# Attention block 0: two halves of one score tile and one transpose tile, side-by-side transposed blocks, and a bias table built head by head

## The chip, the cores and the metric

The kernel runs on one core of a Trainium2 chip, in one launch. Its engines work from separate instruction streams: PE (matmul and transpose), PEld (the weight loads that go with it), DVE and ACT (elementwise work and the only readers of PE's output), POOL, and SP, which in this kernel issues most DMAs. The metric is the device time of one execution in microseconds (us); lower is better.

## The reference

One layer of a hybrid block, 2048 tokens of width 1024, all in float32. One normalised input is projected once; a quarter of the columns goes to a state-space mixer, the rest are q, k and v of 8 heads of 64. The attention sees the token's own chunk of 64 and the 8 chunks before it, with a bias by clipped distance.

```python
h = rmsnorm(x, norm_mix_g[l])
proj = h @ w_in[l]                         # u_ssm (512) | q (512) | k (512) | v (512)
y_ssm = s5_mixer(u_ssm, ...)               # scan over 2048 tokens, 32 groups, 64 complex states
...
rel = jnp.arange(BAND)[None, :] - LEFT_CHUNKS * CHUNK - jnp.arange(CHUNK)[:, None]
idx = jnp.clip(rel, -MAX_REL, MAX_REL) + MAX_REL
bias = rel_bias.astype(jnp.float32)[:, idx]
scores = jnp.einsum('bnqhd,bnkhd->bhnqk', qc, kb).astype(jnp.float32) / math.sqrt(HEAD_DIM)
scores = scores + bias[None, :, None, :, :]
scores = jnp.where(valid[None, None, :, None, :], scores, -1e30)
probs = jax.nn.softmax(scores, axis=-1)
out = jnp.einsum('bhnqk,bnkhd->bnqhd', probs.astype(v.dtype), vb)
```

Both outputs are normalised, joined, projected by `w_out` and added to `x`; a SwiGLU feed-forward layer and a last normalisation follow.

## The kernel before

Float32 accuracy is had from pairs: each operand is split into a high part and a low rest, and a product takes three matmuls (`mm3`, L79). Splitting a weight block is one ACT cast and one DVE or POOL subtraction (L155).

**The first phase** (`u_phase`) projects `u_ssm` for the four token blocks of 512 in the order 1, 2, 3, 0. Its loop variable `n` counts them; step `n` first issues the loads for a block (`prep`: eight `xt` tiles of the transposed input, L441, each split by ACT at L443 and DVE at L444; four rows of `x` for the norm, L450), then runs groups of 24 matmuls, eight tiles by three, on it. `prep` at `n = 2` is the block whose operand tiles are called `raw`, `w`, `xt`, `hi0x` to `hi2x`. The prologue of the state-space part is interleaved.

**The bias table.** `S["nbm"]` lies in DRAM, for each of the 8 heads 128 rows of 640 floats. One DMA from DRAM to DRAM builds it (L522, tile name `nbms<-nbs`), row by row from a one-dimensional list of each head, each row shifted by one float; two more DMAs (L525) overwrite the two masked corners of 64x64 of every head with 1e30. The table is issued at `n = 1`, the corners at `n = 3`. Later each head's 128x640 piece is loaded as the tile `nb` (L801, two buffers), the next head's at the third of a head's four steps.

**The attention phase** (`att_phase`) runs 128 steps: 4 token blocks `sb` x 4 head pairs x 2 heads x 4 query parts `qp` of 128. In each step stand, in this order, the scores of the step (`sc`, L79), the transposes of the step before (`pt`, L82), the value product of a finished head (`pj`), and filling work: generators called units that a table paces over the steps. Units are the projections of q and k (`qk_unit`), of v (`v_unit`), the operands of the next block (`hT_unit`, loads `xt` at L696 with `XB` buffers, product at L706, split at L707 and L708), and 8 `ssm_unit`s in a row, each of them: loads of `U`, `Bst`, `Tm`, `Vm`; matmuls `pj<-U,Bst`; ACT copies into `X` (L574); a scan on POOL (L588 to L600); the copy `XG<-X` issued by POOL (L622); matmuls `pj<-U,Tm` and `pj<-XG,Vm`; ACT copies (L632); eight stores `y<-X` (L635).

A score step is: PE writes `sc`, DVE adds the bias and takes the running minimum (`s<-sc,nb`, then `mn`, both L830), ACT takes the exponential (L833). PE then transposes `s` into `pt`; ACT copies it to `pth` (L848), and DVE makes the rest `ptl` (L849), which the value product reads. In token block 0 step `qp` has only `qp + 1` key blocks, numbered 4 to `qp + 4`; each is put at place `kb % 5` of `pt` and `pth`, so key block 4 is at place 4 and the others at 0 and up, and the copy takes two instructions each on ACT and DVE when `qp > 0`.

In token block 0 the projection weights are loaded in 512 KB pieces (`raw<-in_w_qk`, `raw<-in_w_v`, L675), split, and written back split as 1 MB pieces (`wss<-w`, L686) for the later blocks. `q2h`, `q2l`, `ks` are partition moves and stores of q and k (L750, L751, L756); `v` leaves its PSUM tile at L785 (ACT) and L786 (DVE).

**What sets the order.** Matmuls and transposes stand in the order of the program, pinned by `keep_in_program_order`. ACT, DVE, POOL and SP are ordered by a scheduler with its own estimate; an instruction that is pinned keeps its place among the pinned ones of its engine. SP takes its stream strictly in turn: a DMA whose wait is not over holds all DMAs behind it. Every SP DMA also uses one of eight completion semaphores in rotation and waits until the DMA eight places ahead has landed.

## Time and profile before

| what | value |
|---|---|
| time, median of 3 runs | 2354.85 us (2350.14 to 2355.02) |
| the profiled execution: its own time / its span | 2354.0 us / 2352.2 us |
| mean granted PE clock | 0.970 |
| PE busy, share of the span | 2204.0 us, 94% |
| PEld, DVE, ACT, POOL busy | 1853.1, 1468.7, 1001.3, 1136.5 us |
| DMA, all queues | 434.92 MB, mean 185 GB/s |

The first phase takes the first 140 us or so of the span, the attention phase goes to about 815 us, and the rest is the feed-forward part, which the change does not touch. All times quoted below are in us from the start of the span. In rows of a timeline the first number is the start and the second the duration; in square brackets stands how long the engine sat idle before it and what ended that. In rows of waits: total us, times, longest. A window's row gives its length and, engine by engine, the busy time in it and the number of instructions, then the granted PE clock, the busy share of the DMA engines and GB/s.

### The profile page before, as it was taken

The page shows a single profiled execution, that of the slowest core. Times are in us where ns is not written, and L with a number is a line of the kernel's source. Part 1 is how long each engine was busy: PE and PEld are TensorE (multiplying, and loading weights), DVE is VectorE, ACT ScalarE, POOL GpSimd, SP SyncE. Part 2 cuts the span into 40 slices and gives each one's busy share as a digit, 9 for nine tenths or more (in the row PEclk, how much of TensorE's full clock was granted, in tenths as well). Part 3 has the DMA queues.
Part 4 walks back from the last instruction along what each step waited for, and adds up shares of the span by engine and source line. Part 5 has one row for each costly group of instructions (what it writes and reads, how often), then busy time and mean ns, then how long its engine had stood idle before and what let it go on. Part 6 is the DMA issues. An engine that isn't in the chain of part 4 may idle for free.

```text
span 2352.2 us, 30719 instructions
## 1 busy us (share of the span) xinstructions
PE 2204.0 (94%) x10712; PEld 1853.1 (79%) x10712; DVE 1468.7 (62%) x2229; ACT 1001.3 (43%) x1666; POOL 1136.5 (48%) x1280
## 2 busy tenths in 40 slices
PE   8977799999997899989999998999999989999996
PEld 6766688898986788768888887788888868888886
DVE  6745645656555855746775668766645365579676
ACT  4435545555546642333333334433333343345332
POOL 3237644356551432465555557655555364345442
PEclk9989999999998999989999999999999989999998
DMA  8967776776644434743554646554423287465551
GB/s 275 299 203 251 213 205 178 206 213 189 187 139 135 157 117 148 264 143 117 188 171 157 231 169 243 191 199 165 170 89 119 75 310 261 169 211 184 204 179 72
DMA packets 225331, 434.92 MB, mean 185 GB/s; under 512 B 43480, under 2 KB 70152, under 8 KB 218072
## 3 DMA queue, kind: packets, MB, share of 16 engines
q1 hardware_dynamic: 220312, 418.79, 54.1%
q0 software_dynamic: 4864, 14.17, 2.0%
q8 instruction: 84, 1.38, 0.2%
q14 instruction: 71, 0.58, 0.1%
HBM read 292.88 MB, written 132.15 MB: 181 GB/s over the span
## 4 chain that ended last, share of the span: by engine, by line
PE 57%; DVE 4%; issue 1%; DMA 1%; POOL 1%; ACT 1%; SPq 0%; DVEq 0%; ACTq 0%; POOLq 0%
PE X L79 19%; PE ps L79 17%; PE Y L79 9%; PE big L79 7%; PE W L79 5%; DVE sa L1527 1%; DVE lo L155 1%; DMA lo<-hc 0%; POOL c L155 0%; POOL lo L155 0%; POOL sa L1098 0%; DVE hd L155 0%; DMA hd<-wc 0%; DVE S L1346 0%; ACT hi L155 0%
## 5 line engine op out<-in xcount | busy, mean ns | idle before, releaser
L79 PE MATMUL X<-hi,c 128*128 128x512 f32 x1408 | 450.4, 390 | 8.0 <-POOL c L155 4.0
L79 PE MATMUL ps<-hd,hd 128*128 128x512 f32 (+1 forms) x1968 | 435.1, 384 | 8.0 <-DVE hd L155 4.5
L79 PEld LDWEIGHTS ps<-hd,hd 128*128 128x128 f32 x1968 | 361.4, 191 | 80.4 <-DVE hd L155 4.9
L155 POOL TENSOR_TENSOR c<-S,c 128x512 fp32r<-128x512 f32 x176 | 252.8, 1438 | 245.2 <-ACT c L155 242.9
L79 PEld LDWEIGHTS X<-hi,c 128*128 128x128 f32 x1408 | 264.9, 188 | 65.5 <-POOL c L155 4.4
L155 POOL TENSOR_TENSOR hd<-hd 128x1536 fp32r<-128x1536 f32 (+1 forms) x53 | 188.2, 3556 | 211.2 <-ACT hd L155 196.0
L79 PE MATMUL X<-lo,c 128*128 128x512 f32 x704 | 274.4, 390 | 0.0
L155 POOL TENSOR_TENSOR c<-raw,c 128x512 fp32r<-128x512 f32 x132 | 188.1, 1425 | 130.6 <-ACT c L155 100.1
L155 ACT CAST hd<-hd 128x1536 fp32r<-128x1536 f32 (+1 forms) x106 | 147.3, 1392 | 227.6 <-DMA hd<-hq 162.8
L79 PE MATMUL Y<-hi,c 128*128 128x512 f32 x704 | 228.1, 395 | 14.1 <-DVE u L1368 14.1
L1492 DVE TENSOR_TENSOR acc<-acc,ps 128x512 f32<-128x512 f32 x196 | 129.2, 682 | 89.9 <-PE ps L79 89.8
L79 PEld LDWEIGHTS Y<-hi,c 128*128 128x128 f32 x704 | 134.1, 190 | 44.0 <-DVE u L1368 15.8
L830 DVE CUSTOM_DVE_ANT_0 s<-sc,nb 128x640 f32<-128x640 f32 (+4 forms) x128 | 94.5, 738 | 115.7 <-PE sc L79 104.5
L588 POOL TENSOR_TENSOR st<-X,a 128x128 f32<-128x128 f32 (+2 forms) x136 | 46.7, 343 | 247.2 <-ACT X L574 237.1
L79 PE MATMUL big<-m,woh 128*128 128x512 f32 x512 | 163.5, 401 | 0.2 <-DVE yr L1034 0.2
L79 PE MATMUL pf<-hi,w 128*128 128x512 f32 x416 | 151.8, 416 | 9.0 <-ACT w L155 4.6
L155 ACT CAST c<-S 128x512 fp32r<-128x512 f32 x176 | 109.3, 621 | 114.0 <-PE Y L79 59.5
L79 PEld LDWEIGHTS X<-lo,c 128*128 128x128 f32 x704 | 132.4, 188 | 27.3
L1364 ACT COPY u<-X 128x512 f32<-128x512 f32 x132 | 77.0, 584 | 180.2 <-PE X L79 180.2
L155 ACT CAST c<-raw 128x512 fp32r<-128x512 f32 x132 | 82.1, 622 | 152.6 <-PE Y L79 83.0
L79 PE MATMUL Y<-lo,c 128*128 128x512 f32 x352 | 138.4, 393 | 0.0
L155 DVE TENSOR_TENSOR hd<-hd 128x1536 fp32r<-128x1536 f32 (+1 forms) x53 | 111.6, 2107 | 34.3 <-ACT hd L155 33.9
(450 smaller groups left out, 4701.4 us busy)
## 6 DMA issues: line engine op xcount, KB each, us to landing
w<-wss SPq DMA_DIRECT2D x36, 1024.0 KB, 5.6
hq<-g SPq DMA_DIRECT2D x140, 256.0 KB, 2.1
hd<-hq SPq DMA_DIRECT2D x42, 768.0 KB, 4.5
hd<-wc SPq DMA_DIRECT2D x42, 768.0 KB, 6.1
raw<-in_w_gate SPq DMA_DIRECT2D x44, 512.0 KB, 3.7
raw<-in_w_up SPq DMA_DIRECT2D x44, 512.0 KB, 4.1
wc<-px SPq DMA_DIRECT2D x66, 256.0 KB, 3.1
wss<-w SPq DMA_DIRECT2D x12, 1024.0 KB, 5.9
```

The costliest lines, as they stand in the source:

```text
L79: return self.tc.keep_in_program_order(self.tc.nc.tensor.matmul(*a, **b))
L155: return nc.scalar.copy(hi, raw), (lo_eng or nc.gpsimd).tensor_tensor(lo, raw, f32(hi), op=ALU.subtract)
L588: eng.tensor_tensor(t[:, :, :, :n], src, ar, op=ALU.mult)
L830: nc.vector.tensor_tensor_reduce(s[:, :nk].rearrange("p (a b) -> p a b", a=nch), ps[:, :nch, :half], hd.nb[:, nk - 1 :: -1].rearrange("p ( ...
L1364: nc.scalar.copy(u[:], ps[:])
L1492: V.tensor_tensor(a, a, ps[:], op=ALU.add)
L1527: (nc.gpsimd if m else nc.vector).tensor_tensor(self.sa[m][:, :n], self.sa[m][:, :n], t[:, :n], op=ALU.add)
```

## The change

1. In token block 0 all score steps use one two-bank tile `sc` and take its halves by turns (`qp % 2`); likewise one tile `pt` of eight 128x128 places, of which a step uses one half. Before, each step took a new `sc` and a new `pt` from pools with one buffer.
2. In token block 0 the transposed blocks lie side by side (`place`: key block 4 at place 0), so one ACT and one DVE instruction empty a step's `pt`: 24 instructions fewer on each of ACT and DVE. PE and POOL have as many instructions as before.
3. The bias table is built by heads: heads 0 to 2 in one DMA at `n = 2` of the first phase with their corners at `n = 3`; each of heads 3 to 7 by one DMA at step 0, 4, 8, 12, 16 of the attention phase, and its two corner DMAs two steps later. All are pinned in program order on SP. There are 15 more SP DMAs.
4. The attention's pool `aa` lays out `pth`, `ptl` and six `q2h`, `q2l` buffers first, so `nb` and other tiles lie at other addresses. `corner` moves to a pool that lives longer.
5. The product of `hT_unit` (L706 before) is pinned on DVE.

```diff
+def pinned(k, out, in_):
+    k.tc.keep_in_program_order(k.nc.sync.dma_start(out, in_))
+
+def table(k, S, h0, h1):
+
+    if h0 < H:
+        pinned(k, S["nbm"][h0:h1], bass.AP(S["nb"].tensor, S["nb"].offset + 768 * h0 + 1, [[768, h1 - h0], [1, P], [1, 640]]))
+
+def corners(k, S, h0, h1):
+
+    if h0 < H:
+        for m in range(2):
+            pinned(k, S["nbm"][h0:h1, m * 64 : m * 64 + 64, m * 576 : m * 576 + 64].rearrange("h p c -> p h c"), S["corner"][:].unsqueeze(1).to_broadcast([64, h1 - h0, 64]))
...
             prep(b)
-            if n == 1:
-                corner = k.t(p1, "corner", [64, 64])
-                nc.gpsimd.memset(corner[:], 1e30)
-                nc.sync.dma_start(S["nbm"][:], bass.AP(S["nb"].tensor, S["nb"].offset + 1, [[768, H], [1, P], [1, 640]]))
-            if n == 3:
...
+            if n > 1:
+                (table, corners)[n - 2](k, S, 0, 3)
...
-                nc.vector.scalar_tensor_tensor(xt[:], xt[:], k.gm[:, q : q + 1], S["rsn"][:, ts], op0=ALU.mult, op1=ALU.mult)
+                k.tc.keep_in_program_order(
+                    nc.vector.scalar_tensor_tensor(xt[:], xt[:], k.gm[:, q : q + 1], S["rsn"][:, ts], op0=ALU.mult, op1=ALU.mult))
...
+        two = {}
+
+        def place(sb, kb):
+            return kb % 5 if sb else kb - 4
...
-            ps = k.t(psum2, "sc", [P, 2, 512])
+            if sb:
+                ps = k.t(psum2, "sc", [P, 2, 512])[:]
+            else:
+                if h == qp == 0:
+                    two["sc"], two["pt"] = k.t(psum2, "sc", [P, 2, 512]), k.t(psum, "pt", [P, 8, P], bufs=1)
+                ps = two["sc"][:, qp % 2 : qp % 2 + 1]
...
-            pt = k.t(psum, "pt", [P, 5, P], bufs=1)
+            pt = k.t(psum, "pt", [P, 8, P], bufs=1)[:] if sb else two["pt"][:, qp % 2 * 4 : qp % 2 * 4 + 4]
...
-            runs = [(0, 5)] if sb else ([(4, 5)] if qp == 0 else [(4, 5), (0, qp)])
-            for a, b in runs:
-                nc.scalar.copy(pth[:, a:b, qp, :], pt[:, a:b, :])
-                nc.vector.tensor_tensor(ptl[:, a:b, qp, :], pt[:, a:b, :], f32(pth[:, a:b, qp, :]), op=ALU.subtract)
+            n = 5 if sb else qp + 1
+            nc.scalar.copy(pth[:, :n, qp, :], pt[:, :n, :])
+            nc.vector.tensor_tensor(ptl[:, :n, qp, :], pt[:, :n, :], f32(pth[:, :n, qp, :]), op=ALU.subtract)
...
+        for n in "hl":
+            k.t(aa, f"pt{n}", [P, 5, 4, P], F32R)
+        for n in "hl":
+            for _ in range(3):
+                k.t(aa, f"q2{n}", [P, SB], F32R, bufs=3)
...
+            if s % 4 == 0:
+                table(k, S, s // 4 + 3, s // 4 + 4)
+            if s % 4 == 2:
+                corners(k, S, s // 4 + 3, s // 4 + 4)
```

PE's order is the same row for row. In the rows that follow, numbers behind a tile's name count its uses and differ between the two kernels; a lane `DMAHW..` in a wait is one of SP's eight completion semaphores, `DVE_49` and the like are the engines' own. `x2` stands for two such instructions in a row.

SP in the first phase, where the loads of `n = 2` begin; before:

```order
L450 DMA w_151<-in_x 128x1024
L450 DMA w_152<-in_x 128x1024 x2
L522 DMA nbms_69<-nbs_70 1024x1x640
L441 DMA xt_715<-in_xp 128x512
L441 DMA xt_719<-in_xp 128x512
L441 DMA xt_723<-in_xp 128x512
L441 DMA xt_727<-in_xp 128x512
L450 DMA w_151<-in_x 128x1024
```

and after:

```order
L458 DMA xt_714<-in_xp 128x512
L458 DMA xt_718<-in_xp 128x512
L458 DMA xt_722<-in_xp 128x512
L458 DMA xt_726<-in_xp 128x512
L467 DMA w_153<-in_x 128x1024 x2
L467 DMA w_154<-in_x 128x1024
L458 DMA xt_730<-in_xp 128x512
L467 DMA w_154<-in_x 128x1024
L458 DMA xt_734<-in_xp 128x512
L399 DMA nbms_69<-nbs_70 384x1x640
L458 DMA xt_738<-in_xp 128x512
L458 DMA xt_742<-in_xp 128x512
```

The loads of `n = 2` stood behind the whole table; now six of the eight stand ahead of a table of three heads, and two behind it.

SP at the start of the attention phase, where the first `nb` is loaded; before:

```order
L756 DMA ks_68<-lo2x_1313 128x512
L675 DMA raw_1591<-in_w_qk 128x1024
L686 DMA wss_75<-w_1585 128x2048
L801 DMA nb_1542<-nbms_69 128x640
L801 DMA nb_1629<-nbms_69 128x640
L550 DMA U_1688<-u_64 16x16x64 x8
```

and after:

```order
L768 DMA ks_68<-lo2x_1313 128x512
L399 DMA nbms_69<-nbs_70 128x640
L813 DMA nb_1551<-nbms_69 128x640
L686 DMA raw_1601<-in_w_qk 128x1024
L399 DMA nbms_69<-corner_108 64x64 x2
L813 DMA nb_1640<-nbms_69 128x640
L697 DMA wss_75<-w_1595 128x2048
L561 DMA U_1697<-u_64 16x16x64 x8
```

The first `nb` stood behind a 512 KB load and a 1 MB store; now it stands behind the table piece of head 3, and the load and the store come after it.

SP at the end of the first `ssm_unit`, where the weights of the last `qk_unit` of block 0 are loaded (`raw`, its q and its k piece); before:

```order
L756 DMA ks_68<-k_415_1940 128x512
L756 DMA ks_68<-k_418_1943 128x512
L675 DMA raw_2437<-in_w_qk 128x1024
L675 DMA raw_2442<-in_w_qk 128x1024
L801 DMA nb_2468<-nbms_69 128x640
L696 DMA xt_2513<-in_xt 128x512
L696 DMA xt_2515<-in_xt 128x512
L686 DMA wss_75<-w_2436 128x2048
L696 DMA xt_2597<-in_xt 128x512
L550 DMA U_2446<-u_64 16x16x64
L635 DMA y_65<-X_2378 16x4x256 x8
L550 DMA U_2446<-u_64 16x16x64 x7
```

and after:

```order
L399 DMA nbms_69<-nbs_70 128x640
L646 DMA y_65<-X_2347 16x4x256 x8
L686 DMA raw_2402<-in_w_qk 128x1024
L686 DMA raw_2407<-in_w_qk 128x1024
L561 DMA U_2411<-u_64 16x16x64 x8
L561 DMA Bst_2420<-bsts_71 128x512
L561 DMA Tm_2422<-kts_80 16x4x128 x8
L561 DMA Vm_2431<-vs_72 128x4x128
L399 DMA nbms_69<-corner_108 64x64 x2
L813 DMA nb_2435<-nbms_69 128x640
L707 DMA xt_2478<-in_xt 128x512
L707 DMA xt_2480<-in_xt 128x512
```

The two weight loads, the bias piece of head 5 and the first `xt` loads of the next block stood ahead of the eight stores `y`; now the weights stand behind the stores, and the bias piece and the `xt` loads also behind all loads of the second `ssm_unit`. In the same way the two weight loads of the second `v_unit` (`raw<-in_w_v`) stood ahead of the store `ya_s<-ya` of the first head pair, and now stand behind it.

On PE the second score step of block 0 waits for DVE in both kernels (before `[waits DVE_49,PE_49]`, after `[waits DVE_49]`), and the count it waits for belongs to the same DVE instruction, the running minimum `mn` of the step before, although the second step now writes the other half of the tile. The same holds for the steps and transposes that follow in block 0.

More of the change, by code (lines that the diff above doesn't have):

```diff
@@ L868, in pv_head @@
                 for m, px in ((0, pth), (1, ptl)):
-                    k.ta.matmul(yp[:, a * P : b * P], vt, px[:, kb % 5, a:b, :].rearrange("p a b -> p (a b)"),
+                    k.ta.matmul(yp[:, a * P : b * P], vt, px[:, place(sb, kb), a:b, :].rearrange("p a b -> p (a b)"),
                                      start=n == 0 and m == 0, stop=n == len(kbs) - 1 and m == 1)
@@ L1618, in block_kernel @@
             S["sw"] = k.t(p, "sw", [P, 3, 2, NPR])
+            S["corner"] = k.t(p, "corner", [64, 64])
+            nc.gpsimd.memset(S["corner"][:], 1e30)
             with tc.tile_pool(name="apf", bufs=2, space=bass.MemoryType.PSUM, reuse_waits="tile") as k.pfs:
```

5 lines of the change are left out of this document (1 added, 4 removed).

## The prediction

> **What bounds the kernel now.** The chain that ended last comes first, since it says which engine sets the end:
>
> ```profile
> PE 57%; DVE 4%; issue 1%; DMA 1%; POOL 1%; ACT 1%; SPq 0%; DVEq 0%; ACTq 0%; POOLq 0%
> ```
>
> PE carries it, so the change counts by what it does to PE's waits. PE's order is unchanged, and the change lies in the first 350 us. I therefore read PE's waits there, the first phase (0 to 130, first row) and then the attention's start (130 to 340):
>
> ```profile
> PE ps L79 <- ACT raw L443: 10.4, 2, 7.4
> ...
> PE sc L79 <- DVE mn L830: 13.3, 1, 13.3
> PE pj L79 <- DMA XG<-X: 6.2, 3, 4.7
> PE pt L82 <- DVE ptl L849: 5.3, 5, 1.9
> ```
>
> One wait of 13.3 us for a score step stands out; the rest are small, and the row of `XG` is a scan on POOL, which the change leaves alone. Behind this stretch PE is nearly full (window; busy time of PE second), so time that is won or lost in it is not taken up later:
>
> ```profile
> 340.00:500.00 160.00, 152.88 (x944) 138.25 (x943) 94.12 (x165) 87.59 (x172) 89.00 (x234) 0.98 0.66 198
> ```
>
> **Part 1: the first phase, about -6 us.** The whole table is issued at 36.37 and the loads of the next block behind it; SP's timeline, then ACT's and PE's:
>
> ```profile
> 36.37 0.79 SPq L522 DMA_DIRECT2D nbms<-nbs  x1
> 37.50 16.53 SPq L441 DMA_DIRECT2D xt<-in_xp  x4
> ...
> 63.95 1.38 ACT L443 ACTIVATE raw<-xt,g_mix 128x512 fp32r<-128x512 f32 x2 [14.58 <-DMA xt<-in_xp]
> ...
> 53.79 0.39 PE L79 MATMUL ps<-hi,wul 128*128 128x512 f32 x1
> ...
> 61.27 0.39 PE L79 MATMUL ps<-hi,wul 128*128 128x512 f32 x1
> 64.73 0.50 PE L79 MATMUL ps<-raw,wuh 128*128 128x512 f32 x1 [3.08 <-ACT raw L443]
> ...
> 74.80 1.05 PE L79 MATMUL pp<-ident,no 128*128 128x128 f32 x8
> ```
>
> The first load issued behind the table at 37.50 is used at 63.95, 26.5 us later; ACT was idle 14.6 us for it. From 53.79 to 61.27 PE makes 33 steps, 0.227 us each. The group of 24 on the new block takes from 61.5 to 74.8, 13.3 us, against 24 x 0.227 = 5.4: it loses 7.9. Without a table ahead the loads land long before 61. But two of the eight stand behind a table of three heads. The nearest row for a load with no table ahead is this one of the loads issued from 64 to 90:
>
> ```profile
> DMA to landing us min/median/max: 3.2/5.3/8.0
> ```
>
> The whole table cost 26.5 - 5.3 = 21 us of landing; three eighths make about 8. Issued near 54, the two then land near 67, where PE wants them at 61.5 + 18 x 0.227 = 65.6 and, for the split, a microsecond earlier. That gives back up to 2.4, so the term lies between -7.9 and -5.5. Were the loads late for another reason, it would be 0. I take -6.
>
> **Part 2: the first bias piece, about -9.5 us.** SP, ACT, DVE and PE at the start of the attention, and the time that `nb` takes to land:
>
> ```profile
> 141.15 0.56 SPq L675 DMA_DIRECT2D raw<-in_w_qk  x1
> 144.77 0.32 SPq L686 DMA_DIRECT2D wss<-w  x1
> 145.18 3.38 SPq L801 DMA_DIRECT2D nb<-nbms  x2
> 148.86 10.65 SPq L550 DMA_DIRECT2D U<-u  x8
> ...
> 147.49 0.47 ACT L785 ACTIVATE v<-pf,no 128x256 fp32r<-128x256 f32 x1 [4.01 <-DMA kts<-bc]
> 148.00 0.48 DVE L786 SCALAR_TENSOR_TENSOR v<-pf,no,v 128x256 fp32r<-128x256 f32 x1 [3.26 <-ACT v L785]
> 158.25 0.29 DVE L830 CUSTOM_DVE_ANT_0 s<-sc,nb 128x128 f32<-128x128 f32 x1 [9.76 <-DMA nb<-nbms]
> 158.69 0.55 PE L79 MATMUL sc<-hi2x,hi0x 128*128 128x256 f32 x1 [13.26 <-DVE mn L830]
> ...
> DMA to landing us min/median/max: 2.9/6.0/12.9
> ```
>
> `nb` is issued at 145.18 and takes 12.9 us, the most of all, since 1.5 MB stand ahead of it. In the new order it stands where `raw` is now, at about 141.7, with only the 320 KB piece of head 3 directly ahead. With the median of 6.0 it lands at 147.7. The next thing late is `v`: DVE's instruction at 148.00 stands ahead of the first score step and waits for a DMA that is there at 147.4. So the score starts at 148.5 and PE's second one at about 148.9: 158.69 - 148.9 = 9.8, rounded down to 9.5 since a table piece stands ahead. The bounds are 0 (`nb` takes 12.9 + 4 us after all) and -9.8. What hid behind the stall loses its cover: the eight `U` loads, wanted by PE at 177.5, about 168 in the new order. They are issued from about 150, wait for the 1 MB store ahead of them, and should land near 163; the cover is 4 to 5 us.
>
> A rule of the Trainium skill bears on the rest of this wait. After the stall the granted clock is low for a while (windows; the first number after the length is PE's busy time, the third from the end the clock):
>
> ```profile
> 158.00:162.00 4.00, 3.31 (x17) 3.34 (x18) 0.73 (x4) 1.09 (x4) 0.00 (x0) 0.54 0.69 153
> 162.00:180.00 18.00, 18.00 (x117) 16.37 (x116) 7.78 (x19) 8.22 (x21) 0.00 (x0) 1.00 0.20 44
> ```
>
> Some 3.3 us of work at 0.54 lose about 1.5 us. "TensorE: Matmul & The Clock Gate" of the Trainium skill (Part 1) says that the array goes to half rate after an idle window of about 3.4 us and back after as long a busy one; by it a wait shortened below 3.4 would save that 1.5 as well, and the sum would be 1.5 lower. My wait of 148.9 - 145.3 = 3.6 leaves it standing, and the trace agrees with the recovery time.
>
> **Part 3: one evacuation instead of two, about -1.5 us.** Most of these instructions are 128x128 pieces; for ACT from 140 to 345 (minimum, median, maximum ns):
>
> ```profile
> L848 ACT CAST pth<-pt x61: 242/266/698, 163.8 to 343.6; 128x128 fp32r<-128x128 f32 x40, 128x256 fp32r<-128x256 f32 x8, 128x384 fp32r<-128x384 f32 x8, 128x640 fp32r<-128x640 f32 x5
> ```
>
> A merged instruction keeps its elements and saves at most a 128x128 instruction, about 0.25 us; 24 x 0.25 = 6 us on each of ACT and DVE. PE waits for them in only five places, 5.3 us by the row `pt <- ptl`, and part of that is in token block 1 or is other work ahead on DVE. One chain saves 0.25 on ACT and 0.25 on DVE per wait: 0 to -2.5. I take -1.5.
>
> **Part 4: the two halves, 0.** The second score and the second transpose wait for the same DVE instructions as before, so nothing overlaps that didn't. "PSUM — Partial Sum Buffer" of the Trainium skill (Summary) advises letting the matmul write another bank while one is read, and by it the remaining 3.6 us before the second score could go too. The waits of the new program don't make use of it. New addresses of tiles, the corner tile and the pinned product I also put at 0 (the product waits for its `xt` load either way), within 2 us to either side.
>
> **Part 5: loads that now stand later on SP, about +9.5 us.** Where the first `ssm_unit` ends:
>
> ```profile
> 216.58 0.91 SPq L675 DMA_DIRECT2D raw<-in_w_qk  x2
> 221.19 0.33 SPq L801 DMA_DIRECT2D nb<-nbms  x1
> 221.56 1.00 SPq L696 DMA_DIRECT2D xt<-in_xt  x2
> ...
> 235.77 5.19 SPq L635 DMA_DIRECT2D y<-X  x8
> 241.01 3.37 SPq L550 DMA_DIRECT2D U<-u  x7
> 244.42 3.73 SPq L550 DMA_DIRECT2D Tm<-kts  x8
> ...
> 222.06 1.04 ACT L155 CAST w<-raw 128x1024 fp32r<-128x1024 f32 x1
> 223.14 1.80 DVE L155 TENSOR_TENSOR w<-raw,w 128x1024 fp32r<-128x1024 f32 x1 [0.45 <-ACT w L155]
> 242.43 0.48 PE L79 MATMUL pf<-hi,w 128*128 128x512 f32 x1
> 249.37 0.29 DVE L830 CUSTOM_DVE_ANT_0 s<-sc,nb 128x128 f32<-128x128 f32 x1 [5.13 <-PE sc L79]
> ...
> DMA to landing us min/median/max: 3.7/6.7/8.1
> ```
>
> (the last row is `raw` from 180 to 250). Before, the weights were ready at 224.9 for a use at 242.43. Behind the `y` stores they are issued at 241.0, land 3.7 to 8.1 us later, and the cast and the subtraction take 1.04 and 1.2 to 1.8: PE starts 4.5 to 9.5 late, and I take 6.5. `nb` of head 5 stands behind seven more `U`, `Bst`, eight `Tm` and `Vm` loads. The last two `U` wait for the weights' landing (near 247), so these loads end near 253, and `nb`, issued near 255, lands about 259; it was wanted at 249.37 + 6.5 = 256. That adds 0 to 5, I take 2.5. The `xt` loads of the next block, with it, are just in time for a PE that is already late. The second `v_unit`'s weights fall behind the store at 210.08:
>
> ```profile
> 210.08 0.32 SPq L883 DMA_DIRECT2D ya_s<-ya  x1
> ...
> 212.94 0.48 PE L79 MATMUL pf<-w,hi 128*128 128x256 f32 x2
> ...
> 230.42 1.19 PE L79 MATMUL pj<-XG,Vm 128*128 128x256 f32 x2 [4.69 <-DMA XG<-X]
> ```
>
> They land near 216 and are split near 218, 5 us late; but PE then waits 4.69 less for `XG`, whose scan runs on POOL regardless. I put +0.5, between 0 and 4.
>
> **The sum.** -6 - 9.5 - 1.5 + 6.5 + 2.5 + 0.5 = -7.5 us. Against the profiled execution's own 2354.0 that is 2346.5; it lies 0.85 below the median of the runs, 2354.85, against which I give 2347.3. That is 0.32% faster; about 0.2%, 4.7 us, is what a measurement of this kernel can tell from no change.
>
> **The rivals.**
> *The late loads are covered.* If PE reaches these places with slack, because waits like `XG<-X` shrink by what the weights lose, only the gains stay: -17 + 2 = -15, so 2340. For it speaks that 6.2 us of such waits stand there; against it, that PE at 242.43 waits for nothing and so has no slack to give. Chance 0.16.
> *SP's strict order costs more than is won.* It is the same place, the end of the first `ssm_unit`, at its upper bounds: weights at 9.5 late, the `U` loads that wait for them, then eight `Tm` one after another (3.73 us before), two corner DMAs, and only then `nb`, at up to its 12.9 us of landing. `nb` then lands near 271, 249.37 + 22; with -17 that is +5, 2360. It decides once `nb` of head 5 lands later than 249 + 17 + 5. For it speaks that 12.9 us did occur at a place as crowded; against it, that fewer large stores stand here. Chance 0.26.
> *The gains are eaten near their place.* If `nb` of head 0 is not early, since the table piece ahead of it is slow as the whole table was, part 2 shrinks to some -2, the sum to 0, 2355 (within 0.2%). Chance 0.2.
> *The halves really overlap.* Then -3.6 more, 2343.5. The waits exclude it but for a misreading; 0.03.
>
> **Numbers.** My forecast has the remaining 0.35, with its own range 2342 to 2351. Faster by over 0.2%: 0.30 of it, the covered case and the halves, 0.49 in all. Within 0.2%: 0.05 from the forecast's upper end, the 0.2 above, and 0.02 of the slower rival's lower part, 0.27. Slower: the other 0.24. The range 2338 to 2361 reaches from the covered loads to the slower rival's price.
>
> **What would show it.** The windows 60 to 80 should have PE full up to the group's end (part 1). The wait `sc <- mn` should fall from 13.3 to 3 or 4 (part 2). Waits for `w` and for `nb` near the first `y` stores should appear, 6 and 2 us (part 5); if they are over 12 in all, I am wrong towards slower, and if they are missing, towards faster. The waits `pt <- ptl` should shrink by one to two in all.

## The result: slower by 1%, and the profile after

The changed kernel takes 2378.7 us (median of 4 runs, 2375.06 to 2383.46) against 2354.93 before (4 runs): ratio 1.0105, 95% interval 1.008 to 1.013. The forecast was 2347.3 in a range of 2338 to 2361. The profiled execution has 2380.55 us, its span 2378.8, the mean granted clock 0.963.

The chain of work that ended last, and the busy times, of the changed kernel:

```profile
PE 57%; DVE 2%; DMA 2%; POOL 2%; issue 1%; ACT 1%; DVEq 0%; SPq 0%; ACTq 0%; POOLq 0%
PE 2220.4 (93%) x10712; PEld 1865.8 (78%) x10712; DVE 1473.9 (62%) x2205; ACT 999.8 (42%) x1642; POOL 1140.7 (48%) x1280
```

PE still sets the end. It is busy 16 us longer with as many instructions as before (2220.4 against 2204.0), at a mean granted clock of 0.963 against 0.970. These are PE's waits of the changed kernel from 0 to 130, from 130 to 340, and from 400 to 600:

```profile
PE ps L79 <- ACT hi1x L460: 8.6, 1, 8.6
PE ps L79 <- ACT raw L460: 7.5, 1, 7.5
...
PE sc L79 <- DVE mn L852: 17.9, 4, 10.8
PE pf L79 <- ACT w L155: 9.3, 3, 4.5
PE pf L79 <- ACT hi L719: 7.4, 4, 3.2
...
PE pf L79 <- ACT hi L719: 5.3, 4, 1.6
```

Four of them answer to the prediction's places: a wait for `hi1x` in the group that was to be full; the score's wait for `mn`, 10.8 where 3.6 was expected; waits for `w` in the attention, expected; and waits for `hi`, an operand of the next block, at 400 to 600, where the kernel before has only this of that kind:

```profile
PE pf L79 <- DVE lo L708: 0.2, 1, 0.2
```

PE's instructions stand in the same order in all these kernels, so each matmul can be followed from one trace to the other. The table gives how much later (+) or earlier the same matmul starts than in the kernel before; the column's head is its start there. The last five rows are experiments, told below.

| kernel | 70 us | 76 | 120 | 158.7 | 251 | 303 | 577 | 800 |
|---|---|---|---|---|---|---|---|---|
| forecast |  | -6 | -6 | -15.5 |  | -7.5 | -7.5 | -7.5 |
| changed | -6.6 | +2.8 | +2.8 | +0.3 | +8.3 | +15.7 | +22.8 | +23.7 |
| before, product pinned (`e4_pin`) | +2.6 | +1.8 | +2.0 | +1.3 | +1.4 | +5.8 | +11.2 | +12.6 |
| changed, product not pinned (`e5_nopin`) | -6.9 | +1.3 | +1.3 | -1.6 | +7.8 | +12.6 | +13.1 | +13.4 |
| the same, table by rows (`q4_e5rows`) | -5.7 | -7.4 | -5.7 | -3.3 | -3.4 | +3.9 | +1.0 | +2.0 |
| changed, table by rows (`q1_rows`) | -6.7 | -4.6 | -4.6 | -1.8 | +0.7 | +12.3 | +18.0 | +18.2 |
| before, merged copies, early first bias (`f5_nb0xt`) | -1.2 | -1.9 | -1.4 | -13.0 | -15.2 | -15.6 | -14.9 | -14.0 |

So the 24 us come in pieces. The first is at 70 to 76 us, where 9.4 are lost, 8.6 of them at one matmul. Timeline of the changed kernel, SP, ACT and PE:

```profile
52.81 0.85 SPq L399 DMA_DIRECT2D nbms<-nbs  x1
54.65 10.22 SPq L458 DMA_DIRECT2D xt<-in_xp  x4
...
72.70 0.72 ACT L460 ACTIVATE hi1x<-xt,g_mix 128x512 fp32r<-128x512 f32 x1 [13.29 <-DMA xt<-in_xp]
...
73.48 0.80 PE L79 MATMUL ps<-hi1x,wuh 128*128 128x512 f32 x1 [8.59 <-ACT hi1x L460]
```

The load issued behind the table of three heads at 54.65 is used at 72.70, 18 us later, where 13 had been allowed. The second is the first bias piece; timeline of SP, POOL, DVE and PE:

```profile
145.41 2.53 SPq L399 DMA_DIRECT2D nbms<-nbs  x1
147.99 1.37 SPq L813 DMA_DIRECT2D nb<-nbms  x1
...
143.29 1.14 POOL L298 DMA_DIRECT2D bsts<-vg  x2
...
158.63 0.29 DVE L852 CUSTOM_DVE_ANT_0 s<-sc,nb 128x128 f32<-128x128 f32 x1 [9.41 <-DMA nb<-nbms]
...
158.98 0.58 PE L79 MATMUL sc<-hi2x,hi0x 128*128 128x256 f32 x1 [10.85 <-DVE mn L852]
```

SP came to `nb` at 147.99, later than before (145.18), not at 141.7. The third is the end of the first `ssm_unit`:

```profile
210.28 0.57 SPq L813 DMA_DIRECT2D nb<-nbms  x1
...
211.84 2.58 SPq L686 DMA_DIRECT2D raw<-in_w_v  x2
...
238.84 4.93 SPq L646 DMA_DIRECT2D y<-X  x8
243.81 0.90 SPq L686 DMA_DIRECT2D raw<-in_w_qk  x2
...
216.84 0.58 PE L79 MATMUL sc<-k,q2h 128*128 128x256 f32 x1 [4.74 <-DVE mn L852]
...
248.88 0.50 PE L79 MATMUL pf<-hi,w 128*128 128x512 f32 x1 [3.14 <-ACT w L155]
```

The weights stand behind the eight stores as the order said. The bias piece at 210.28 is that of head 3, which stood at 193.41 before; the prediction had not looked at it. The fourth is the stretch from 251 us on, which holds the products of `hT_unit`: the changed kernel loses 7.4 from 251 to 303 and 7.1 more up to 577. Not all of this is the pin, since `e5_nopin`, without it, also loses 4.8 from 251 to 303, though only 0.5 from there to 577.

### The profile page after: what moved, and what is told of

It reads as the page before. It is cut to its first block, busy times and chain, and to the rows that moved or that the text cites. A ratio compares the mean times of both kernels' runs of the same rounds, so it can differ in the third digit from the quotient of the medians.

```text
span 2378.8 us, 30686 instructions
## 1 busy us (share of the span) xinstructions
PE 2220.4 (93%) x10712; PEld 1865.8 (78%) x10712; DVE 1473.9 (62%) x2205; ACT 999.8 (42%) x1642; POOL 1140.7 (48%) x1280
## 4 chain that ended last, share of the span: by engine, by line
PE 57%; DVE 2%; DMA 2%; POOL 2%; issue 1%; ACT 1%; DVEq 0%; SPq 0%; ACTq 0%; POOLq 0%
PE X L79 19%; PE ps L79 18%; PE Y L79 9%; PE big L79 7%; PE W L79 5%; DVE lo L155 1%; DMA hd<-wc 1%; POOL c L155 0%; DMA lo<-hc 0%; POOL lo L155 0%; POOL sa L1128 0%; DMA acc<-x 0%; ACT hi L155 0%; DVE S L1376 0%; POOL sa L1127 0%
## 5 line engine op out<-in xcount | busy, mean ns | idle before, releaser
L855 ACT ACTIVATE s<-s,mn 128x640 f32<-128x640 f32 (+4 forms) x128 | 97.9, 765 | 84.3 <-DVE mn L852 83.6
```

The lines of the kernel that those rows point to most:

```text
L855: nc.scalar.activation(s[:, :nk], s[:, :nk], AF.Exp, bias=mn[:], scale=-1.0, accum_out=sums[sb, pr][:, hh, qp : qp + 1])
```

## The experiments

### The change in parts

`e1_table`: the kernel before with only the table by heads (part 3 of the change). `e2_evac`: with only the two-bank tiles and the blocks side by side (parts 1 and 2). `e6_evaclayout`: this and the pool's layout (part 4). `e4_pin`: with only the pinned product (part 5). `e5_nopin`: the changed kernel without it.

```diff
+                k.tc.keep_in_program_order(
-                nc.vector.scalar_tensor_tensor(xt[:], xt[:], k.gm[:, q : q + 1], S["rsn"][:, ts], op0=ALU.mult, op1=ALU.mult)
+                nc.vector.scalar_tensor_tensor(xt[:], xt[:], k.gm[:, q : q + 1], S["rsn"][:, ts], op0=ALU.mult, op1=ALU.mult))
```

(`e4_pin`; `e5_nopin` is the reverse on the changed kernel.)

> Before plus the head-by-head bias table alone (with its corner tile); scores, transposes, layout and the product of hT_unit as before. Theory A (table pieces on SP): most of the 24 us comes from here, +10 to +20 us against before, with a wait near 8 us for hi1x in the first phase, the first score still waiting some 10 us for nb, and waits for w near 213 and 243. Theory B (the pinned product of hT_unit does most): within 4 us of before. Theory C (merged evacuation or two-bank tiles): within 4 us of before.

> Before plus the two-bank score and transpose tiles and the side-by-side blocks alone. Theories A and B: -3 to 0 us, the waits of pt for ptl shrink by 1 to 2 us, nothing else moves. Theory C: +5 us or more, with new waits of sc or pt for DVE in block 0.

> Before with the merged evacuation, the two-bank tiles and the new layout of the pool aa; the table as before, no pin. Its instruction order differs from before only in the merged instructions and four places on SP. If these parts do no harm by themselves (theory A): -3 to +1 us against before. If the addresses matter (the first nb no longer waits for a matmul): the wait for mn falls by some us and the time by 3 us or more.

> Before plus the pinned product of hT_unit on DVE alone. Theory B: +10 us or more, with waits of pf for hi near the starts of token blocks 1, 2 and 3 of some 5 us each. Theory A: 0 to +5 us, since the product waits for its xt load either way. Theory C: 0.

> After without the pin of hT_unit's product, all else as after. Theory A: 0 to -5 us against after, so +19 to +24 against before. Theory B: -10 us or more against after, the waits of pf for hi at the later token blocks gone. If table and pin each have a part (as the shift of PE's instructions suggests: about +10 by 260 us, the rest at the hi waits), about -12 against after.

| kernel | median us | ratio to the kernel before, 95% interval |
|---|---|---|
| `e1_table` | 2372.22 | 1.0087 (1.0065 to 1.0109) |
| `e2_evac` | 2353.16 | 1.0002 (0.9988 to 1.0016) |
| `e6_evaclayout` | 2355.13 | 1.0003 (0.9991 to 1.0014) |
| `e4_pin` | 2363.87 | 1.0048 (1.0027 to 1.0068) |
| `e5_nopin` | 2365.76 | 1.0060 (1.0040 to 1.0081) |

The halves, the merged copies and the layout do nothing by themselves. The table by heads costs 18 us alone (2372.2 against 2354.2) and 12 together with these parts (`e5_nopin`). The pin costs 10 alone and 10 to 13 in the changed kernel: 10.3 by the table of shifts at 800 us, 12.9 by the medians. Why the table costs 6 more alone is not known; the two kernels part between 251 and 303 us, where the same matmuls slip by 11.0 in `e1_table` and by 4.8 in `e5_nopin`. PE's waits of `e1_table` from 0 to 130 and 130 to 340, which are like those of the changed kernel, then the waits for `ptl` of `e2_evac` from 130 to 340, which are those of before, then of `e4_pin` from 400 to 600:

```profile
PE ps L79 <- ACT hi1x L460: 10.4, 1, 10.4
...
PE sc L79 <- DVE mn L841: 19.1, 4, 11.3
```

```profile
PE pt L82 <- DVE ptl L858: 5.2, 4, 2.3
```

```profile
PE pf L79 <- ACT hi L708: 4.9, 5, 1.5
```

Why the pin costs: the product group of `hT_unit` in the window 215 to 320 of the kernel before, then of `e4_pin` (times ns minimum, median, maximum, and first and last start):

```profile
L706 DVE SCALAR_TENSOR_TENSOR xt<-xt,g_mix,rsn x13: 735/752/968, 225.5 to 308.6; 128x512 f32<-128x512 f32 x13
```

```profile
L707 DVE SCALAR_TENSOR_TENSOR xt<-xt,g_mix,rsn x8: 741/749/982, 254.7 to 286.3; 128x512 f32<-128x512 f32 x8
```

Before, 13 of them ran here: the eight of block 1, the first at 225.5, and five of block 2, some 100 us ahead of the use of block 2 at 427. Pinned, only the eight of block 1 run, the first 29 us later, and those of block 2 wait for their place in the program, just ahead of their use. At the start of blocks 1, 2 and 3 PE then waits for `hi`, and by the table `e4_pin` loses 4.4 us from 251 to 303 and 5.4 from 303 to 577. The price of one product has not changed, only how far ahead the scheduler may put it.

### Why the first phase lost

`k2_latetable` is `e5_nopin` with the table of heads 0 to 2, and its corners, behind all loads of the first phase. `g1_acttable` is the kernel before with the whole table on ACT's queue, where it is issued at 7.62 us. `j1_actq` is `e5_nopin` with all table and corner DMAs on ACT's queue, not pinned, which puts them at 7.8 to 155 us. `m1_split` is `e6_evaclayout` with heads 0 and 1 at `n = 1` on SP, and heads 2 to 7 in one DMA, with their corners, on ACT's queue at steps 1 and 3 of the attention.

```diff
-            if n > 1:
-                (table, corners)[n - 2](k, S, 0, 3)
+            if n == 3:
+                table(k, S, 0, 3)
+                corners(k, S, 0, 3)
```

(`k2_latetable`.)

> The kernel after without the pin, and with the table of heads 0 to 2 and its corners issued behind all input loads of the first phase instead of between the loads of n = 2. Theory A1 (the two input loads behind that table make the first phase late): the wait of 8.4 us for hi1x goes, the first phase ends about 8 us earlier, and the time is 5 to 9 us below the kernel without the pin (some +4 against before). Rival (the loads are late from DMA load whatever stands ahead): the wait stays above 5 us and the time within 2 us.

> Before, but the whole table in one piece is issued by ACT's queue at the same place. Theory A1 (loads wait in SP's queue behind the table): the loss at the first group of n = 2 (7.9 us) falls to 0 to 4 us, time -4 to -8 us against before. Rival (the table's traffic itself takes the DMA engines, whichever queue it is in): the loss stays, time within 2 us.

> The kernel after without the pin, and with all table and corner DMAs issued by ACT's queue instead of SP's, unpinned. Theory A3 (the pieces on SP push the weight loads, the nb of heads 3 and 5 and the input loads back in SP's strict order): the waits for w near 213 and 243 us and for mn near 212 us (some 11 us together) go, and the time is 6 to 12 us below the kernel without the pin. Rival (the pieces cost by their DMA traffic or by the scheduler's other choices): the waits stay, time within 3 us. In the first phase the loads no longer stand behind the table in one queue; that may add another gain of up to 8 us.

> The kernel of the first of these runs, with the table of heads 0 and 1 where the whole table is before, and that of heads 2 to 7 in one piece with its corners on ACT's queue, pinned at steps 1 and 3 of the attention phase, where the DMA engines are two tenths busy. Theory A1 (the input loads wait for the table's bytes): the loss of 7.9 us at the first group of n = 2 goes and no new one comes, since only 0.66 MB stand ahead; -5 to -9 us against before. Rival (any cut of the table only moves the loss to another place, as in the two kernels before): within 3 us, with new waits of 5 us or more before 130.

| kernel | median us | ratio to the kernel before, 95% interval |
|---|---|---|
| `k2_latetable` | 2362.81 | 1.0057 (1.0038 to 1.0076) |
| `g1_acttable` | 2378.06 | 1.0116 (1.0094 to 1.0139) |
| `j1_actq` | 2369.57 | 1.0084 (1.0065 to 1.0103) |
| `m1_split` | 2371.97 | 1.0068 (1.0045 to 1.0091) |

In `k2_latetable` the same matmul as in the 76 us column is 11.7 us earlier than before, so the table ahead of loads is the cause; the loads behind it in turn were late for the weights, and at 120 us all was given back. PE's waits from 0 to 130:

```profile
PE pf L79 <- DVE w L155: 3.6, 1, 3.6
PE pf L79 <- DVE us L500: 3.0, 1, 3.0
```

`g1_acttable` and `j1_actq` say nothing on this question. In both the order on SP changed: the load `bbg<-bbs` went ahead of most loads of the first phase, and its wait for POOL's stores `bbs` held SP's stream, for 22.7 us in `j1_actq`. The row of `g1_acttable`, from SP's waits from 0 to 40:

```profile
SPq L372 <- DMA bbs<-bbi: 24.4, 1, 24.4
```

`m1_split` was the puzzle: with three quarters of the table gone it still was 1.3 us late at 76 us. I had taken that for proof that the phase is bound by its bytes. The share of the DMA engines behind the table's issue says otherwise. Windows of the changed kernel (three heads), of `m1_split` (two heads) and of `g1_acttable` (eight heads); the last two numbers are the DMA engines' mean share and GB/s. The fourth fence shows `m1_split` again, later, where its table of heads 2 to 7 (six heads) runs from ACT's queue: the window, and what that queue moved in it (packets, MB, share of 16 engines):

```profile
70.00:73.00 3.00, 0.00 (x0) 0.00 (x0) 0.00 (x0) 0.30 (x1) 0.00 (x0) 0.50 0.20 77
```

```profile
60.00:64.00 4.00, 1.01 (x2) 0.69 (x3) 1.32 (x2) 2.07 (x4) 0.00 (x0) 0.94 0.13 50
```

```profile
18.00:29.00 11.00, 0.00 (x0) 0.00 (x0) 9.26 (x82) 1.15 (x2) 0.58 (x1) 0.50 0.53 198
```

```profile
176.00:187.00 11.00, 4.58 (x22) 3.46 (x20) 1.40 (x5) 2.12 (x5) 0.00 (x0) 0.97 0.38 147
...
q10 hardware_dynamic: 635, 1.62, 37.7%
```

PE waits for a load while the DMA engines are a fifth busy. Of 16 engines, 0.20 is 3.2, 0.13 is 2.1, 0.53 is 8.5: about as many engines as heads, at some 25 GB/s each. In the first two windows the table was issued 17 and 25 us earlier, so part of what moves there are the waiting loads' own shares on the table's engines. In the fourth no other queue has a packet, and 0.377 of 16 is 6.0 engines for six heads. The Trainium skill ("DMA: Bandwidth & Descriptors", the section on why a DMA increments its semaphore by 16) says that a DMA is spread over the largest number of engines up to 16 that divides its slowest dimension, dimensions of size 1 left out; its section on queues, rings and completion order says that each engine consumes its descriptors in order. The windows agree with the first, since the table's slowest dimension is the head, and the 18 us of the load behind the three-head table agree with the second. One head's 327,680 bytes then take 13 us on its one engine, an estimate at 25 GB/s, whether the DMA holds two, three or eight heads, and every load behind it has a share on the same engines. A piece of a single head has its 128 rows as slowest dimension. The one that the changed kernel issues at 172.7 lands in 4.0 us, too fast for one engine at 25 GB/s (`nbms` from 165 to 180):

```profile
DMA to landing us min/median/max: 4.0/4.0/4.0
```

The test turns the dimensions round, rows first, with the same bytes to the same places: in the changed kernel (`q1_rows`), in `e5_nopin` (`q4_e5rows`), in the kernel before (`q2_beforerows`, whole table) and in `f5_nb0xt`, below (`q3_f5rows`).

```diff
-pinned(k, S["nbm"][h0:h1], bass.AP(S["nb"].tensor, S["nb"].offset + 768 * h0 + 1, [[768, h1 - h0], [1, P], [1, 640]]))
+pinned(k, S["nbm"][h0:h1].rearrange("h p c -> p h c"), bass.AP(S["nb"].tensor, S["nb"].offset + 768 * h0 + 1, [[1, P], [768, h1 - h0], [1, 640]]))
```

> The changed kernel with the list of a table DMA's dimensions turned round: rows first, heads second, the same bytes to the same places. In the changed kernel PE waits 8.6 us for hi1x while the DMA engines are 0.20 busy and move 77 GB/s (70 to 73 us); with a table of two heads the same wait shows about 50 GB/s, of six heads some 150, of eight some 205, so about 25 GB/s for each head. Theory A (one DMA engine for each head): the three-head table runs on three engines for 320 KB / 25 GB/s = 13 us, as long as the whole table on eight, and loads behind it wait for these three. With rows first it spreads over all engines: the wait of 8.6 us for hi1x goes to 0 to 2, the stretch to 80 us is 5 to 8 earlier, and if the rest stays, the time falls by 3 to 8 from 2378.7 to about 2373. Theory B (the loads wait for the bytes of the table, as I read it before): the wait stays at 7 to 9 and the time at 2379 within 3. The Trainium skill (DMA: Bandwidth & Descriptors, the section on why a DMA increments its semaphore by 16) says that a DMA is split over the largest number up to 16 that divides its slowest dimension; by it 3 heads mean 3 engines, 128 rows 16: theory A.

> The changed kernel without the pinned product (2365.8 us), with rows first in the table's DMA. Theory A: the first phase gains 5 to 8 us and the time falls to 2358 to 2362; what is left above the kernel before is then the loads behind table pieces and stores in the attention. Theory B: 2366 within 3.

> The kernel before with rows first in the whole table's DMA, nothing else. Theory A: eight engines become sixteen, the 13 us of the table become about 6.5, the loads behind it land some 6 us sooner, and PE's loss of 7.9 us at 61 to 75 us shrinks to 1 to 4; 2348 to 2353 if later loads don't take it back. Theory B: the bytes are the same and the engines were 0.9 busy over 48 to 60 us, so nothing moves: 2354 within 3.

> The fastest kernel so far (the kernel before with the merged evacuation and the first head's bias loaded early, 2340.8 us) with rows first in the table's DMA. Theory A: another 2 to 6 us, 2335 to 2339. Theory B: 2341 within 3.

| kernel | median us | ratio to the kernel before, 95% interval |
|---|---|---|
| `q1_rows` | 2372.95 | 1.0093 (1.0080 to 1.0106) |
| `q4_e5rows` | 2357.19 | 1.0022 (1.0010 to 1.0034) |
| `q2_beforerows` | 2350.75 | 0.9992 (0.9980 to 1.0005) |
| `q3_f5rows` | 2341.36 | 0.9961 (0.9949 to 0.9973) |

The first theory holds in the first phase. PE's waits of `q1_rows` from 0 to 130 and 130 to 340, and its window 60 to 80:

```profile
PE ps L79 <- ACT hi1x L460: 1.8, 1, 1.8
...
PE sc L79 <- DVE mn L852: 18.2, 3, 16.1
...
60.00:80.00 20.00, 17.88 (x75) 14.35 (x74) 13.72 (x32) 11.85 (x19) 2.20 (x4) 0.91 0.85 285
```

The wait falls from 8.6 to 1.8, the DMA engines move 285 GB/s in that window, and by the table of shifts the stretch to 76 us is 4.6 earlier than before in `q1_rows`, 7.4 in `q4_e5rows`, 6.3 in `q2_beforerows`. What is kept of it differs. In `q1_rows` and `q4_e5rows` the scheduler, which goes by its own estimate, also put SP's DMAs in another order: at the first bias piece `raw` and the 1 MB store went ahead of `nb` again, and PE waits 16.1 and 15.7 us there. In `q2_beforerows` DVE's order changed, PE waits 1.8 us for `us`, and of 6.3 some 4 are left in the profiled run, while the medians show no difference. On top of `f5_nb0xt`, where 2 to 6 us were expected, nothing is gained: `q3_f5rows` is 6.8 earlier than the kernel before at 76 us, where `f5_nb0xt` is 1.9 earlier, but 14.8 against 13.0 at 158.7 and 14.6 against 14.0 at 800.

### The first bias piece

`f5_nb0xt` is `e6_evaclayout` with the first head's bias loaded ahead of the attention's units into a free `xt` buffer, 512 of its 640 columns, which is all that token block 0 reads. `p1_nb0` is the same edit on `e5_nopin`, `m2_split_nb0` on `m1_split`. `k4_latestore` is `e6_evaclayout` with three 1 MB stores `wss<-w` behind the first two `nb` loads.

```diff
+        nbs[0] = k.t(aw, "xt", [P, SB], bufs=XB)
+        nc.sync.dma_start(nbs[0][:], S["nbm"][0][:, :SB])
         v0 = v_unit(0, 0)
```

> The same, with the first head's bias (512 of its 640 columns, all that token block 0 reads) loaded into a free xt buffer, so that it stands ahead of the 512 KB load, the 1 MB store and POOL's four 512 KB stores. The prediction's part 2 (the place in the queue makes the first nb late): the wait of sc for mn falls from 13.3 to 3 to 5 us, -8 to -10 us against before. Theory A2 (the DMA engines are full from 140 on whatever the order): the wait stays at 8 us or more, the time within 4 us.

> The kernel after without the pin, and with the first head's bias loaded early into a free xt buffer. If the first nb's lateness is worth as much here as it was without the table pieces: the wait of sc for mn falls from 9.9 to 2 us, -8 us against the kernel without the pin, so about +3 against before. If the later waits (the weights, the nb of heads 3 and 5) are bound to DMAs and POOL's scan that don't come earlier with PE: -4 or less.

> Both together: the split table on two queues and the early first bias. If the two gains are independent: -12 to -18 us against before. If the first phase's gain is taken up by the first nb (which waits for DMA traffic and not for PE): -8 to -10.

> Before with the merged evacuation and the new layout (not the table change, not the pin), and with the three 1 MB weight stores of the first v_unit and of the second qk_unit moved behind the first two nb loads on SP. Theory A2 (the first nb is late because the DMA engines are full of other transfers, whoever stands directly ahead): the wait of sc for mn falls from 13.3 to 3 to 6 us; against before -4 to -9 us if the U loads behind the stores still come in time, less if they don't. Rival (nb is late for its own place in the queue or the DRAM table): the wait stays above 10 us, the time within 3 us.

| kernel | median us | ratio to the kernel before, 95% interval |
|---|---|---|
| `f5_nb0xt` | 2340.78 | 0.9944 (0.9926 to 0.9962) |
| `p1_nb0` | 2366.38 | 1.0048 (1.0031 to 1.0065) |
| `m2_split_nb0` | 2360.37 | 1.0028 (1.0015 to 1.0041) |
| `k4_latestore` | 2347.56 | 0.9984 (0.9968 to 0.9999) |

Timeline of `f5_nb0xt`, SP, DVE and PE:

```profile
139.73 0.57 SPq L905 DMA_DIRECT2D xt<-nbms  x1
...
145.37 0.29 DVE L840 CUSTOM_DVE_ANT_0 s<-sc,xt 128x128 f32<-128x128 f32 x1 [1.59 <-DMA xt<-nbms]
...
145.73 0.39 PE L79 MATMUL sc<-hi2x,hi0x 128*128 128x256 f32 x1 [1.62 <-DVE mn L840]
```

Issued at 139.73, it is used 5.6 us later, at 145.37; PE's wait of 13.26 becomes 1.62, and the 13 us are kept to the end. This kernel is faster than both. In `p1_nb0` SP reaches the same load only here:

```profile
145.30 2.24 SPq L916 DMA_DIRECT2D xt<-nbms  x1
```

That is behind the moves `ks` and, in time, behind all four of POOL's 512 KB stores `bsts`, which start here at 143.04 to 145.22; the wait is 7.3 and the time that of `e5_nopin`. `k4_latestore` takes the stores away from ahead of `nb`: the wait becomes 9.7, between the two forecasts, and the time 0.16% less, so these stores are a part of the cause and not all of it. What separates the early piece from the late ones in these kernels is whether it is issued ahead of the crowd at 143 us; POOL's stores themselves were not moved. `m2_split_nb0` is 11.6 us faster than `m1_split`, the same gain.

### The loads in the attention

`n2_actpieces` is `e5_nopin` with the pieces of heads 3 to 7 on ACT's queue at their steps, and their corners seven steps behind the piece instead of two.

```diff
-    k.tc.keep_in_program_order(k.nc.sync.dma_start(out, in_))
+    k.tc.keep_in_program_order(eng.dma_start(out, in_))
```

(`eng` is ACT's queue for heads 3 to 7.)

> The kernel after without the pin, with the table pieces of heads 3 to 7 at the same steps but on ACT's queue, and their corners there one step later (pinned), so that the same bytes move at the same times but stand in no order on SP. Theory A3 (SP's order): the waits for w near 213 and 243 us and for mn near 212 us go; PE is no later at 260 us against 160 us than before (after without the pin it loses 9 us there); time 6 to 12 us below that kernel, if waits of ACT for its own DMAs don't take it back. Rival (the traffic of the pieces): these waits stay at 8 us or more together, time within 3 us.

It takes 2373.04 us (1.0075, 1.0058 to 1.0092). Its waits for `w` and for the bias of head 3 are gone, but PE comes 23 us late to that place, so this alone doesn't show why. PE's waits from 130 to 340, and in the same view of `m1_split`:

```profile
PE pt L82 <- DVE ptl L869: 26.1, 4, 13.2
```

```profile
PE pt L82 <- DVE ptl L867: 23.9, 6, 21.0
```

In both, DVE stands still in front of `ptl`, because the product of `hT_unit` stands ahead of it there and waits for its `xt` load. In `m1_split` this load is late because of SP, and in `n2_actpieces` in part: a `Tm` load, which has no data in common with the table, waits until the table piece on ACT's queue has landed. By the trace the two use the same completion semaphore, so ACT's DMAs take theirs from SP's rotation. A row of SP's waits and one of DVE's timeline, of `m1_split` (160 to 200) and of `n2_actpieces` (160 to 240):

```profile
SPq L559 <- DMA nbms<-nbs: 23.6, 1, 23.6
...
199.92 1.64 DVE L715 SCALAR_TENSOR_TENSOR xt<-xt,g_mix,rsn 128x512 f32<-128x512 f32 x2 [17.99 <-DMA xt<-in_xt]
```

```profile
SPq L561 <- DMA nbms<-nbs: 5.4, 1, 5.4
...
194.84 0.88 DVE L717 SCALAR_TENSOR_TENSOR xt<-xt,g_mix,rsn 128x512 f32<-128x512 f32 x1 [11.33 <-DMA xt<-in_xt]
```

In `m1_split` ACT stands still too; its timeline:

```profile
193.10 5.85 ACTq L407 DMA_DIRECT2D nbms<-corner  x2
199.00 3.01 ACT L583 COPY X<-pj 64x256 f32<-64x256 f32 x8 [19.95 <-DMA raw<-in_w_qk]
```

ACT does no work from 179 to 199, and the two corner DMAs stand in that gap. By their semaphores the first waits for SP's `Vm` load and the second for its `raw` load, as the row says. Both are loads that SP issued late. The table piece had landed by 187.6, when SP went on. So both kernels pay for the shared semaphores and say nothing on SP's order.

Other rows answer the question instead. In the changed kernel the weights that SP issues at 243.81 land 4.0 and 6.1 us later, within the 3.7 to 8.1 of the kernel before; they are late by their place in the stream and not by a slower transfer. In `j1_actq`, where no piece is left in SP's stream, PE is not late by more at 303 us (+16.6) than at 158.7 (+18.7), and waits for no weights at 243. And in `q1_rows` and `q4_e5rows` the scheduler put the weights ahead of the stores again. SP's timeline of `q1_rows`:

```profile
216.78 2.09 SPq L686 DMA_DIRECT2D raw<-in_w_qk  x2
...
236.77 4.85 SPq L646 DMA_DIRECT2D y<-X  x8
```

There is no wait for these weights there, and from 158.7 to 251 PE loses 2.5 us in `q1_rows` and nothing in `q4_e5rows`, where the changed kernel loses 8.0 and `e5_nopin` 9.4. The pieces in these two kernels hold one head each and have the same slowest dimension as before, so it is the order and not the form of the pieces that differs.

Behind 251 us time is lost again, in kernels without the pin too: up to 303 us 7.3 in `q4_e5rows`, 11.6 in `q1_rows` (with the pin). Longer waits for `hi` are a part of it; the row of `q4_e5rows` from 248 to 310, then of the kernel before from 251 to 303:

```profile
PE pf L79 <- ACT hi L718: 6.8, 3, 4.3
```

```profile
PE pf L79 <- ACT hi L707: 4.4, 2, 2.4
```

Which loads or instructions cause this loss was not tested.

## Why the prediction was wrong, point by point

**What bounds the kernel, and where to look:** right. PE's order is the same, PE sets the end, and in the kernels without the pin what is lost or won by 303 us stays to the end of the attention within 2.4 us.

**Part 1, the first phase (-6): failed.** The gain was there, -6.6 at 70 us. The step that failed is the price of the two loads behind the smaller table: "three eighths make about 8", that is, a delay by bytes. `q1_rows` and `q4_e5rows` show that it goes by engines: three heads occupy three DMA engines for the same 13 us as eight heads occupy eight. The give-back was 9.4 where 2.4 was the bound. The prediction's window 60 to 80 was the right witness; PE is busy there for 11.4 us instead of 20. With rows first the part comes to -4.6 and -7.4, about what was forecast.

**Part 2, the first bias piece (-9.5): failed on the issue time.** "It stands where `raw` is now, at about 141.7" took a row's place in the order for a time. SP reached it at 147.99. The moves `ks` ahead of it started 2.8 later than before (142.61 against 139.80), as late as PE itself was after part 1's loss, and took 1.4 longer to issue; the table piece then took 2.53 us to issue. By then POOL's 2 MB were under way, so `nb` was there 10.6 us later (158.63 - 147.99) instead of 6. The shift from 120 to 158.7 was -2.5. The mechanism and its size were right, as `f5_nb0xt` shows with -11.6 over the same stretch. The rival "gains are eaten near their place" named this, with the table piece as the culprit, and put -2 on it. (One reading in this part is slightly off: PE's stall before began at 158.69 - 13.26 = 145.43, so the wait that was to be left is 3.5 and not 3.6. Nothing came to hang on it.)

**Part 3, one evacuation (-1.5):** nothing, within 0.14% (`e2_evac`). PE's waits for `ptl` are as long as before.

**Part 4, halves, addresses and the pinned product (0 within 2): failed, and the largest miss.** The halves and the layout are 0 (`e6_evaclayout`). The pin costs 10 to 13 us (10.3 by the shifts at 800 us; 12.9 by the medians, 2378.7 - 2365.8). "The product waits for its `xt` load either way" saw the wait and not the place: without the pin five of eight products of a later block ran some 100 us before their use. The row with x13 in the window 215 to 320 was in the trace before, and the working made no use of it.

**Part 5, later SP loads (+9.5):** right in size and mostly in mechanism, by luck in its sum: from 158.7 to 260 the changed kernel loses 10.3 us (+0.3 to +10.6). The weights of `qk_unit` were 3 us late instead of 6.5, since PE itself came later, and the bias of head 5 cost 1 instead of 2.5. What was missed is the bias of head 3, 4.7, and the second `v_unit`'s weights, 1.72 and 1.67 of waiting and some 2.7 lost between and behind these waits, at a granted clock of 0.50 from 217 to 222 and 0.65 from 222 to 227, where 0.5 stood. The shorter wait for `XG` gave 4.9 back at 230.42, as the prediction said it would. The prediction also called the `xt` loads of the next block just in time. Without the pin 3.0 more are lost between 260 and 303 (`e5_nopin`, +9.6 to +12.6), at the waits for `hi` and `lo` (8.6 us against 5.7 before); the cause stays open.

**The sum:** -7.5 was forecast, +23.8 measured. Of the 31 us between, about 9 are part 1, 7 part 2, 1.5 part 3, 1 part 5, and 13 what is lost behind 260 us (+10.6 to +23.7). Of these 13 the pin is some 9, since `e5_nopin` loses 3.8 there as well (+9.6 to +13.4). The slower rival put the loss on `nb` of head 5, where it is not; none of the rivals held the pin or the three engines.

What is left open: `q4_e5rows`, without the pin and with the table by rows, is still 0.2% slower than the kernel before, with a wait of 15.7 us for the first bias and the loss of 7.3 from 251 to 303. That it would win with that piece early, as `f5_nb0xt` does, was not tried.

## What to carry to other kernels

Before an edit that pins an instruction is put at nothing, count in the trace how many of its instances run ahead of their place in the program: that lead is what the pin takes away. Before a DMA is cut or moved, look at its outermost dimension and at the DMA engines' share while something waits for it: a wait beside idle DMA engines can mean a transfer on a few of them. Here fewer heads did not mend that, another place moved the loss further on (`k2_latetable`), and another order of dimensions took the wait away. A place in an issue order becomes a time only when everything ahead of it in that queue is summed up, with its waits, and what the other queues start in the meantime.

## What the runs showed of the hardware that was not expected

- With a table DMA of two, three or eight heads on the engines, about 50, 77 and 198 GB/s were moved in all, with 0.13, 0.20 and 0.53 of the DMA engines busy; six heads alone took 6.0 engines and moved 147 GB/s (`m1_split`). A load behind the three-head table was used 18 us after its issue. With 128 rows as the outermost dimension the wait behind it fell from 8.6 to 1.8 us.
- The issue of a table piece of one head took 2.53 us of SP at 145.41 (head 3, its row stands above) and 0.54 at 214.46 (head 6, row below). The DMA engines were 0.96 busy from 145 to 148 and 1.00 from 214 to 215, so their share does not tell the price; what does stays open:

```profile
214.46 0.54 SPq L399 DMA_DIRECT2D nbms<-nbs  x1
```

- A DMA on ACT's queue held SP's stream for 23.6 us, through a completion semaphore that both queues use, and two DMAs in ACT's own stream, which waited for late loads of SP, stopped ACT's work for 19.95 us (`m1_split`).
